# A load that is sent later and four warming products fewer, at the start of a hybrid encoder layer

## The chip, the cores and the metric

The kernel runs on one core of a Trainium2 chip. The metric is the device time of one execution in microseconds (us): 418.63 us, the median of three executions before the change (417.64 to 419.09). TensorE is called PE here, VectorE DVE, ScalarE ACT, GpSimd POOL and SyncE SP.

## The reference

One step of a streaming encoder layer for two groups of rows, 256 of a prompt and 32 of a running stream, all with the same weights. One projection of x feeds every branch:

```python
p = x @ w_in                                  # x: 288 x 1024 in all, w_in: 1024 x 11848
(qa, ka, va, oa, za, ia, fa, qb, kb, vb, zb, qi, ki, wi, ga, gb) = jnp.split(p, cuts, axis=-1)
...
score = jnp.einsum('bqh,bqhs->bqs', wi * (IDX_HEADS ** -0.5), jax.nn.relu(sc))   # sc: qi against ki
_, idx = lax.top_k(score, k_sel)
...
mixed = jax.nn.sigmoid(ga) * (branch_a @ w_out_a) + jax.nn.sigmoid(gb) * (branch_b @ w_out_b)
return layer_norm(DN_ALPHA * x + mixed @ w_o, ln_g, ln_b)
```

Branch A is an mLSTM with a matrix memory of 4 heads, branch B a sparse attention of 8 heads over the keys that the index scores pick. The change touches neither: it lies in the first microseconds, in the first part of `x @ w_in`.

## The kernel before

The weights come in tiles of 128 output columns (`ORDER` lists them). A weight tile is 128 partitions by 1024 float32. ACT rounds it to a high part (`wh`), DVE subtracts to get the low part (`wl`), and PE multiplies in three passes (high by high, high by x's low part, low by high), each 8 times over the 1024 rows of the sum in blocks of 128.

The first five tiles (the small tile `sm` and the four `qi` tiles) are handled apart, because they are what the start waits for. Their data and x come packed by block: for each of the 8 blocks k, `first[:, k]` holds 288 columns of x and then 5 x 128 weight columns, 928 in all. `lead[k]` is its place in SBUF. Block 0 comes in two pieces, cut behind the first weight tile (`cut` = 288 + 128 = 416 columns):

```python
    sp.dma_start(lead[0][:, 0:cut], a["first"][:, 0, 0:cut])
    act.dma_start(lead[0][:, cut:LEAD], a["first"][:, 0, cut:])
    for k in range(1, KT):
        sp.dma_start(lead[k][:, 0:LEAD], a["first"][:, k])
```

The first piece and the seven whole blocks go through SP's queue (q1 in the profile), the second piece through ACT's (q10). `first_products` (line 993 holds its one product) then runs, for every block, over the five tiles. Block 0 is multiplied as plain float32 from `lead[0]` as it landed, without splitting. The product with tile 0 reads the first piece alone, those with tiles 1 to 4 read the weights of the second piece and x of the first. Blocks 1 to 7 are split first (lines 181 to 192) and multiplied in three passes of five products.

Ahead of that PE runs `WARM` = 16 products of a zeroed tile (`warm`, bfloat16, 256 columns) whose result nobody reads (line 160). DVE clears that tile first (line 155).

Each engine executes its instructions in the order in which the program records them; what stands in one engine's queue waits for what is ahead of it. DMAs are issued in the order of the queue of the engine that issues them, and such an issue may carry a wait for another engine. The DMAs take eight semaphores in turn (DMAHW0 to DMAHW7); the ninth DMA waits until the first one's has been reached.

Of the kernel before, what the change touches and what calls it, by code (L numbers as in the profile page):

```python
# [12 lines left out]
BF = mybir.dt.bfloat16  # L13
# [12 lines left out]
BH, BD = 8, 128  # L26
IH, ID = 8, 64
CHUNK = 64
WARM = 16
MID = 4  # L30
FIRST = 5
LEAD = T + 128 * FIRST
# [55 lines left out]
def body(ctx, tc, a, o):  # L88
    nc = tc.nc
    pe, act, dve, pool, sp = nc.tensor, nc.scalar, nc.vector, nc.gpsimd, nc.sync  # L90
# [5 lines left out]
    def sb(name, shape, dt=F32, tag=None, bufs=1):  # L96
        return P.tile(shape, dt, name=name, tag=tag or name, bufs=bufs)

    def bank(name, n=512):
        return ps.tile([128, 512], F32, name=name, tag="side", bufs=6)  # L100
# [50 lines left out]

    xh = sb("xh", [128, KT, T], F32R)
    xl = sb("xl", [128, KT, T], F32R)
    warm = sb("warm", [128, 256], BF)
    dve.memset(warm, 0.0)
    wp = bank("warm_p")

    def keep_warm(n):
        for _ in range(n):
            pe.matmul(wp[:, :256], lhsT=warm[:, :128], rhs=warm, start=True, stop=True)  # L160

    keep_warm(WARM)

    early = sb("early", [128, 2064], tag="v1l")
# [5 lines left out]
    lead = [sb(f"wst_k{k}", [128, KT * 128], tag="wst", bufs=8) for k in range(KT)]  # L170
    cut = T + 128
    sp.dma_start(lead[0][:, 0:cut], a["first"][:, 0, 0:cut])
    act.dma_start(lead[0][:, cut:LEAD], a["first"][:, 0, cut:])
    for k in range(1, KT):
        sp.dma_start(lead[k][:, 0:LEAD], a["first"][:, k])
# [1049 lines left out]
```

## Time and profile before

| | us |
|---|---|
| median of the three timed executions | 418.63 (417.64 to 419.09) |
| the profiled execution, whole | 418.94 |
| its span, first to last instruction | 417.1 |
| PE busy | 410.7 (98% of the span) |
| DVE, ACT, POOL busy | 315.6, 214.6, 201.8 |
| DMA moved | 78.89 MB, mean 189 GB/s |

The span is what the trace covers; the 1.84 us that the whole execution takes beyond it are not in the trace. PE's busy share counts the warming products too. Times in the trace's rows are from the span's start.

### The profile page before, as it was taken

The page shows a single profiled execution, that of the slowest core. Times are in us where ns is not written, and L with a number is a line of the kernel's source. Part 1 is how long each engine was busy: PE and PEld are TensorE (multiplying, and loading weights), DVE is VectorE, ACT ScalarE, POOL GpSimd, SP SyncE. Part 2 cuts the span into 40 slices and gives each one's busy share as a digit, 9 for nine tenths or more (in the row PEclk, how much of TensorE's full clock was granted, in tenths as well). Part 3 has the DMA queues.
Part 4 walks back from the last instruction along what each step waited for, and adds up shares of the span by engine and source line. Part 5 has one row for each costly group of instructions (what it writes and reads, how often), then busy time and mean ns, then how long its engine had stood idle before and what let it go on. Part 6 is the DMA issues. An engine that isn't in the chain of part 4 may idle for free.

```text
span 417.1 us, 8481 instructions
## 1 busy us (share of the span) xinstructions
PE 410.7 (98%) x3145; PEld 392.9 (94%) x3145; DVE 315.6 (76%) x633; ACT 214.6 (51%) x408; POOL 201.8 (48%) x466
## 2 busy tenths in 40 slices
PE   8999999999999999999999999999999999999995
PEld 7999999999999998779999999999999999998864
DVE  4669999987887596778898788897565466666674
ACT  5776465344845565567554556455434333535402
POOL 0200049995288856857920164766615448710031
PEclk9999999999999999999999999999999999999999
DMA  8987878779844720448535643444555547444014
GB/s 308 394 286 224 285 238 295 274 194 330 308 145 152 242 91 0 166 145 306 172 122 163 234 135 128 150 154 152 194 160 158 193 153 263 158 152 126 25 48 143
DMA packets 32948, 78.89 MB, mean 189 GB/s; under 512 B 11644, under 2 KB 15084, under 8 KB 32108
## 3 DMA queue, kind: packets, MB, share of 16 engines
q1 hardware_dynamic: 32044, 77.05, 55.5%
q10 hardware_dynamic: 864, 1.32, 1.0%
q8 instruction: 24, 0.39, 0.4%
q14 instruction: 16, 0.13, 0.1%
HBM read 72.45 MB, written 7.81 MB: 192 GB/s over the span
## 4 chain that ended last, share of the span: by engine, by line
PE 97%; DVE 1%; POOLq 0%; ACT 0%; DVEq 0%; issue 0%
PE pj L930 25%; PE pj L931 25%; PE pj L932 24%; PE yn L974 5%; PE pj L993 4%; PE vap L946 1%; PE pj L948 1%; PE vap L953 1%; PE vap L947 1%; PE pj L947 1%; PE vap L948 1%; PE pj L946 1%; PE warm_p L160 1%; PE yn L978 1%; PE ix L406 1%; PE os L544 0%
## 5 line engine op out<-in xcount | busy, mean ns | idle before, releaser
L930 PE MATMUL pj<-xh,wh 128*128 128x288 f32 x640 | 189.2, 296 | 0.0
L931 PE MATMUL pj<-xl,wh 128*128 128x288 f32 x640 | 188.9, 295 | 0.0
L932 PE MATMUL pj<-xh,wl 128*128 128x288 f32 x640 | 188.6, 295 | 0.0
L149 DVE TENSOR_TENSOR wl<-wst,wh 128x1024 fp32r<-128x1024 f32 x112 | 138.0, 1234 | 28.0 <-ACT wh L142 27.6
L142 ACT CAST wh<-wst 128x1024 fp32r<-128x1024 f32 x112 | 117.4, 1048 | 22.8 <-PE pj L931 6.8
L930 PEld LDWEIGHTS pj<-xh,wh 128*128 128x128 f32 x640 | 120.3, 188 | 1.4 <-issue 1.3
L931 PEld LDWEIGHTS pj<-xl,wh 128*128 128x128 f32 x640 | 120.3, 188 | 0.0
L932 PEld LDWEIGHTS pj<-xh,wl 128*128 128x128 f32 x640 | 120.3, 188 | 0.0
L117 POOL COPY pt<-bm 32x96 f32<-32x96 f32 x128 | 50.4, 394 | 20.3 <-DVE bm L584 15.1
L117 POOL COPY kaT<-kn 32x128 f32<-32x128 f32 x64 | 32.1, 502 | 22.8 <-DVE kn L681 20.3
L117 POOL COPY hn<-qaT 32x128 f32<-32x128 f32 x48 | 24.1, 502 | 17.4 <-DVE qaT L657 10.2
L117 POOL COPY vn<-qaT 32x128 f32<-32x128 f32 x64 | 28.0, 438 | 2.6
L891 ACT ACTIVATE sg<-pj 128x288 f32<-128x288 f32 x16 | 6.6, 411 | 26.1 <-PE pj L932 26.1
L932 PE MATMUL pj<-bah,wl 128*128 128x288 f32 x64 | 18.9, 296 | 0.0
L931 PE MATMUL pj<-bbl,wh 128*128 128x288 f32 x64 | 18.9, 296 | 0.0
L931 PE MATMUL pj<-bal,wh 128*128 128x288 f32 x64 | 18.9, 295 | 0.0
L930 PE MATMUL pj<-bah,wh 128*128 128x288 f32 x64 | 18.8, 294 | 0.0
L932 PE MATMUL pj<-bbh,wl 128*128 128x288 f32 x64 | 18.8, 294 | 0.0
L930 PE MATMUL pj<-bbh,wh 128*128 128x288 f32 x64 | 18.8, 293 | 0.0
L738 POOL TENSOR_TENSOR dd<-dd,mhalf 128x2 f32<-128x2 f32 x4 | 5.4, 1350 | 24.6 <-DVE dd L737 24.4
L1024 POOL TENSOR_TENSOR nr<-mv,mhalf 128x1 f32<-128x1 f32 (+1 forms) x3 | 4.0, 1349 | 24.3 <-DVE mv L1023 24.3
L824 ACT CAST mxh<-sg 128x288 fp32r<-128x288 f32 x8 | 3.5, 433 | 22.7 <-DVE sg L904 22.7
(465 smaller groups left out, 717.8 us busy)
## 6 DMA issues: line engine op xcount, KB each, us to landing
wst<-in_w SPq DMA_DIRECT2D x112, 512.0 KB
wst_k<-in_first SPq DMA_DIRECT2D x7, 464.0 KB
rscr<-rrow SPq DMA_DIRECT2D x2, 768.0 KB
out_k<-kbT SPq DMA_DIRECT2D x1, 1152.0 KB
stC<-in_state_C SPq DMA_DIRECT2D x1, 1028.0 KB
out_C_sample<-stC SPq DMA_DIRECT2D x1, 1028.0 KB
bm<-rscr SPq DMA_DIRECT2D x1, 1024.0 KB
ckT<-in_cache_k SPq DMA_DIRECT2D x1, 1024.0 KB
```

What stands on the lines that cost most here:

```text
L117: pool.tensor_copy(out(quads[k], quads[i]), turned(quads[i], quads[k]))
L142: act.copy(split[t][0], stage[t])
L149: dve.tensor_tensor(wl, stage[t], wh.bitcast(F32), OP.subtract)
L891: act.activation(sg, q, AF.Sigmoid)
L930: pe.matmul(p[:, :T], lhsT=wh[:, c], rhs=h[:, k], start=(k == 0), stop=False)
L931: pe.matmul(p[:, :T], lhsT=wh[:, c], rhs=l[:, k], start=False, stop=False)
L932: pe.matmul(p[:, :T], lhsT=wl[:, c], rhs=h[:, k], start=False, stop=(k == KT - 1))
L946: pe.matmul(banks[i], lhsT=xh[:, k, r], rhs=wh[:, c], start=(k == 0), stop=False)
L947: pe.matmul(banks[i], lhsT=xh[:, k, r], rhs=wl[:, c], start=False, stop=False)
L948: pe.matmul(banks[i], lhsT=xl[:, k, r], rhs=wh[:, c], start=False, stop=(k == KT - 1))
L974: pe.matmul(p, lhsT=x[:, k, r], rhs=w[:, c], start=first and i == 0, stop=last and i == 2)
L993: pe.matmul(p[t][:, new], lhsT=w[:, 128 * t:128 * t + 128], rhs=x[:, new], start=(k == 0), stop=(k == KT - 1 and w is wl))
```

## The change

The warming products read a constant of ones that POOL sets in the program's preamble, and there are 12 of them. DVE's first instruction no longer clears `warm` (which is gone) but the place of the second piece in `lead[0]`; since the second piece is then written to the same place, its DMA, in ACT's queue, waits for DVE.

```diff
-WARM = 16
+WARM = 12
...
-    warm = sb("warm", [128, 256], BF)
-    dve.memset(warm, 0.0)
     wp = bank("warm_p")
+    ones = nc.const_aps.tensor(1.0, (128, 256), BF)

     def keep_warm(n):
         for _ in range(n):
-            pe.matmul(wp[:, :256], lhsT=warm[:, :128], rhs=warm, start=True, stop=True)
+            pe.matmul(wp[:, :256], lhsT=ones[:, :128], rhs=ones, start=True, stop=True)
...
     sp.dma_start(lead[0][:, 0:cut], a["first"][:, 0, 0:cut])
+    dve.memset(lead[0][:, cut:LEAD], 0.0)
     act.dma_start(lead[0][:, cut:LEAD], a["first"][:, 0, cut:])
```

ACT's queue at the program's start, before (`wst_k0` is `lead[0]`, `wst_k1` is `lead[1]`; the words in brackets are the semaphores that an instruction waits for):

```order
L173 DMA wst_k0_88<-in_first 128x512
L182 ACT_TABLE_LOAD
L182 CAST xh_65<-wst_k0_88 128x288 [waits DMAHW1_49]
L182 CAST xh_65<-wst_k1_89 128x288 [waits DMAHW2_49]
L191 CAST wh_k1_107<-wst_k1_89 128x384
```

And with the change:

```order
L173 DMA wst_k0_82<-in_first 128x512 [waits DVE_49]
L182 ACT_TABLE_LOAD
L182 CAST xh_65<-wst_k0_82 128x288 [waits DMAHW0_49]
L182 CAST xh_65<-wst_k1_83 128x288 [waits DMAHW1_49]
L191 CAST wh_k1_102<-wst_k1_83 128x384
```

The order is the same; the issue of the second piece has a wait for DVE, and the table load and the casts stand behind it. The first piece's semaphore is now DMAHW0 instead of DMAHW1.

PE's queue where the warming products end and block 0 begins, before:

```order
L160 LDWEIGHTS warm_67
L160 MATMUL warm_p_69<-warm_67 128x256
L993 MATMUL pj0_190<-wst_k0_88 128x288 [waits DMAHW1_49]
L993 MATMUL pj1_191<-wst_k0_88 128x224 [waits DMAHW0_49]
L993 MATMUL pj2_192<-wst_k0_88 128x224
L993 MATMUL pj3_193<-wst_k0_88 128x224
L993 MATMUL pj4_194<-wst_k0_88 128x224
L993 MATMUL pj0_190<-xh_65,wh_k1_107 128x288 [waits DVE_49,Activation_49]
```

And with the change:

```order
L159 LDWEIGHTS const-bfloat16-1.0
L159 MATMUL warm_p_67<-const-bfloat16-1.0 128x256
L993 MATMUL pj0_185<-wst_k0_82 128x288 [waits DMAHW0_49]
L993 MATMUL pj1_186<-wst_k0_82 128x224 [waits DMAHW2_49]
L993 MATMUL pj2_187<-wst_k0_82 128x224
L993 MATMUL pj3_188<-wst_k0_82 128x224
L993 MATMUL pj4_189<-wst_k0_82 128x224
L993 MATMUL pj0_185<-xh_65,wh_k1_102 128x288 [waits DVE_49,Activation_49]
```

The product with tile 0 waits for the first piece, the one with tile 1 for the second, in both; twelve pairs of a weight load and a product stand ahead of them instead of sixteen, and the first of these no longer waits for DVE.

SP's queue, which has the first piece and the blocks, with the change:

```order
L171 DMA wst_k0_82<-in_first 128x416
L175 DMA wst_k1_83<-in_first 128x928
L175 DMA wst_k2_84<-in_first 128x928
L175 DMA wst_k3_85<-in_first 128x928
L175 DMA wst_k4_86<-in_first 128x928
L175 DMA wst_k5_87<-in_first 128x928
L175 DMA wst_k6_88<-in_first 128x928
L175 DMA wst_k7_89<-in_first 128x928 [waits DMAHW0_49]
L131 DMA wst5_145<-in_w 128x1024 [waits DMAHW1_49,DMAHW2_49,DVE_49,PE_49]
```

The last block's load waits for DMAHW0 in both; that was the second piece's semaphore before and is the first piece's now. The first weight tile behind it (`wst5`) also waits for PE, which must have read `lead[0]`, whose place it takes.

## Rows read from the trace of the kernel before

**Rows 1.** The page: busy time and share of each engine (busy us, share of the span, instructions), and the chain that ended last, by engine.

```profile
PE 410.7 (98%) x3145; PEld 392.9 (94%) x3145; DVE 315.6 (76%) x633; ACT 214.6 (51%) x408; POOL 201.8 (48%) x466
...
PE 97%; DVE 1%; POOLq 0%; ACT 0%; DVEq 0%; issue 0%
```

**Rows 2.** All waits of PE in the whole span (us in total, times, longest), and busy time by stretch: the stretch, its length, then PE, PEld, DVE, ACT and POOL busy us with instructions, granted clock, DMA share, GB/s.

```profile
PE warm_p L160 <- DVE warm L155: 1.1, 1, 1.1
...
7.30:19.40 12.10, 12.10 (x106) 12.10 (x105) 9.67 (x15) 9.10 (x15) 1.19 (x10) 1.00 1.03 394
19.50:100.00 80.50, 80.50 (x640) 80.17 (x639) 71.64 (x164) 43.63 (x87) 40.75 (x92) 1.00 0.81 262
100.00:200.00 100.00, 100.00 (x797) 92.47 (x796) 77.22 (x170) 61.26 (x141) 66.55 (x168) 1.00 0.53 182
200.00:300.00 100.00, 100.00 (x776) 98.08 (x776) 83.50 (x174) 52.24 (x92) 49.79 (x100) 1.00 0.49 159
300.00:405.00 105.00, 104.92 (x764) 98.93 (x764) 64.71 (x97) 43.01 (x65) 40.47 (x88) 1.00 0.44 142
```

**Rows 3.** The start in order of time: start us, length us, engine, line, what, how many, and in brackets how long the engine had been idle and what ended it.

```profile
0.38 0.10 POOL L1203 MEMSET const-bfloat16-1.0<- 128x1 bf16 x1
...
0.80 0.41 ACTq L173 DMA_DIRECT2D wst_k<-in_first  x1
0.81 0.40 SPq L172 DMA_DIRECT2D wst_k<-in_first  x1
0.90 0.17 DVE L155 MEMSET warm<- 128x128 uint32 x1 [0.90 <-PEq L1203]
...
1.12 3.60 PE L160 MATMUL warm_p<-warm 128*128 128x256 bf16 x16 [1.12 <-DVE warm L155]
1.25 1.28 ACT L182 ACT_TABLE_LOAD   x1 [1.25 <-PEq L1203]
1.27 3.56 SPq L175 DMA_DIRECT2D wst_k<-in_first  x7
4.34 0.43 ACT L182 CAST xh<-wst_k 128x288 fp32r<-128x288 f32 x1 [1.81 <-DMA wst_k<-in_first]
```

**Rows 4.** PE's products one by one, from the last warming product to the first of block 1 (start us, length us as modelled with its end; the starts are what is read).

```profile
4.30 0.42 PE L160 MATMUL warm_p<-warm 128*128 128x256 bf16 x1
4.51 0.69 PE L993 MATMUL pj<-wst_k 128*128 128x288 f32 x1
5.00 0.69 PE L993 MATMUL pj<-wst_k 128*128 128x288 f32 x1
5.48 0.58 PE L993 MATMUL pj<-wst_k 128*128 128x224 f32 x1
5.85 0.58 PE L993 MATMUL pj<-wst_k 128*128 128x224 f32 x1
6.22 0.60 PE L993 MATMUL pj<-wst_k 128*128 128x224 f32 x2
6.47 0.54 PE L993 MATMUL pj<-wst_k 128*128 128x224 f32 x2
6.66 0.54 PE L993 MATMUL pj<-wst_k 128*128 128x224 f32 x2
6.85 0.54 PE L993 MATMUL pj<-wst_k 128*128 128x224 f32 x2
7.26 0.46 PE L993 MATMUL pj<-xh,wh_k 128*128 128x288 f32 x1
```

**Rows 5.** The length of DVE's memsets: all of line 155 (one, ns minimum, median and maximum), and line 300's by shape (busy us, mean ns).

```profile
L155 DVE MEMSET warm<- x1: 165/165/165, 0.9 to 0.9; 128x128 uint32 x1
...
L300 DVE MEMSET gt<- 4x576 f32 x1 | 0.5, 538 | 0.1
```

**Rows 6.** What the two DMA queues had moved by 2.9 us and by 3.5 us (packets, MB, share of 16 engines), with q1 the queue of SP and q10 that of ACT.

```profile
q1 hardware_dynamic: 65, 0.11, 16.1%
q10 hardware_dynamic: 43, 0.09, 14.3%
...
q10 hardware_dynamic: 103, 0.21, 22.1%
q1 hardware_dynamic: 123, 0.20, 20.4%
```

**Rows 7.** Stretches of the start (columns as in rows 2), for the DMA rate in the last column and the granted clock ahead of the DMA share.

```profile
1.80:2.40 0.60, 0.60 (x5) 0.41 (x4) 0.00 (x0) 0.60 (x1) 0.00 (x0) 1.00 0.86 127
2.40:2.90 0.50, 0.50 (x4) 0.38 (x3) 0.00 (x0) 0.13 (x1) 0.00 (x0) 1.00 0.73 240
3.40:3.90 0.50, 0.50 (x5) 0.33 (x3) 0.00 (x0) 0.00 (x0) 0.00 (x0) 1.00 1.14 428
4.40:5.60 1.20, 1.20 (x5) 0.91 (x4) 0.46 (x1) 0.37 (x1) 0.00 (x0) 1.00 1.06 424
```

**Rows 8.** SP's load of the last block, which waits for the second piece's semaphore, and the preparation of block 1 (ACT and DVE) in order of time.

```profile
4.50 0.33 SPq L175 DMA_DIRECT2D wst_k<-in_first  x1
...
5.61 0.43 ACT L182 CAST xh<-wst_k 128x288 fp32r<-128x288 f32 x1 [0.84 <-DMA wst_k<-in_first]
5.95 0.51 ACT L191 CAST wh_k<-wst_k 128x384 fp32r<-128x384 f32 x1
```

## The prediction

> **What bounds the kernel now.** I read the page first: PE is busy for 98% of the span and makes up 97% of the chain that ended last [rows 1]. Then PE's own waits: there is one in the whole span, the 1.12 us before its first product, and by stretch PE is busy without a break to 300 us and for 104.92 of the next 105 us [rows 2]. So every instruction of PE starts when the one before it lets it, and a shift of PE's work at the start is carried to the end, unless something that does not move with PE catches up with it. The other engines' work is released by PE (buffers come free when PE has read them), so it moves along. What counts is the moment at which PE is through with block 0.
>
> Then the start in order of time [rows 3]. SP and ACT issue the two pieces at 0.81 and 0.80. DVE clears the warming tile from 0.90, PE begins at 1.12 and runs 16 products; the starts of the first and the last are (4.30 - 1.12) / 15 = 0.212 us apart each [rows 3, 4]. The first piece has landed by 4.34, when ACT, idle until then, begins its cast [rows 3]. PE begins block 0 at 4.51, that is 0.21 after its last warming product: here it is the products that hold PE back, by 0.17 us, and not the data. The second piece had landed by 4.50, since SP's load of the last block, which waits for that semaphore, goes out then [rows 8]; PE wants it only at 5.48, behind the product with tile 0 (two entries of 0.49 us) [rows 4].
>
> The third thing is PE's clock. The product with 224 columns starts 0.37 us after the one before at 5.85 and at 6.22, and 0.19 us at 6.66 and 6.85 [rows 4]: the lower and the higher of the two levels, 1.2 and 2.4 GHz, with the rise between 6.22 and 6.47; I take 6.3. (The granted clock in the stretches reads 1.00 throughout [rows 7]; the products' own distance says otherwise, and I go by it.) PE had been busy without a break for 5.2 us when the clock rose. Until the rise, a microsecond gained at the start is worth half a microsecond at the end, because the work brought forward is then done at half rate.
>
> **The change part by part.**
>
> *The constant.* The wait for DVE goes. The constant is set by POOL at 0.38, before the barrier [rows 3], so PE can start when the barrier lets it: not before 0.80, where ACT and SP start, and not after 1.12. I take DVE's 0.90. A product of 128x256 that reads one column over and over is not in the trace; it costs 0.212 us if it goes like the zeroed tile's, and could cost 0.25 before the next step is touched.
>
> *Four products fewer.* 12 x 0.212 = 2.54 us from 0.90: PE is free at 3.45 instead of 4.51.
>
> *The memset.* 128 elements took 165 ns and 576 took 538 [rows 5]: 0.83 ns for one more, so 512 take about 0.48 us. DVE ends at 1.38 and ACT's issue, at 0.80 before, goes out at about 1.45: 0.65 us later. DVE's next work was at 4.80, behind ACT's cast; nothing is queued there that waits. On ACT the table load stands behind the issue: from 1.25-2.53 it moves to about 1.9-3.2. The cast of the first piece, at 3.7 at the earliest below, covers that; were the cover gone, the cast would feed only block 0's split x, which no product of block 0 reads. On SP nothing is queued behind the new wait. The last block's load now waits for the first piece instead of the second, so it goes out no later, and behind six blocks it finds DMA at its full rate [rows 7].
>
> *The first piece alone.* By 2.9 us the two queues had moved 0.11 and 0.09 MB, by 3.5 us 0.20 and 0.21 [rows 6]; the first piece is 0.213 MB, so it was through at about 3.55. Now the second begins 0.65 later, at about 2.6. If SP's queue alone then gets what both got, it has 127 GB/s x 0.6 us + 240 x 0.2 = 0.124 MB at 2.6 [rows 7]; for the other 0.09 MB it gets half of some 300 GB/s and needs 0.6 us: 3.2, or 0.35 earlier, and the landing moves from 4.34 to 4.0. The ends: no gain at all, 4.34, if a single queue is no faster alone; and 0.6 us, 3.7, if it shares nothing. I take 4.0. PE then waits from 3.45 to 4.0 and does tile 0 until 4.97.
>
> *The second piece.* It starts 0.65 later and now meets block 1 in SP's queue. Between 2.9 and 3.5 the queues moved 58 and 60 packets [rows 6], the same number; block 1's rows are 928 x 4 = 3712 bytes against 512 x 4 = 2048, so ACT's queue should get 2048 / 5760 = 36% of 0.42 MB/us, 0.15. At 3.2 it has about 0.09 of its 0.262 MB; the rest takes 1.15 us, to 4.35. Before, by the same arithmetic (0.21 at 3.5, then 55% of 0.428 [rows 7]), it ended at 3.7 and landed at 4.50. That is later by 0.65, the whole delay; if it keeps half of the rate it is through at 4.0, later by 0.3. I take 0.6, near the first: landed at 5.1. The ends are 4.5, no later than before, and 5.3. Block 1 itself had to share with the second piece in both kernels, so that its landing (ACT's cast at 5.61 [rows 8]) stays where it is.
>
> *The sum.* PE begins tile 1 at the later of 4.97 and 5.1, so at 5.1 instead of 5.48: 0.38 earlier. With the clock's rise at 6.3 as before that is worth half: 0.19 us, say 0.2. With the ends: a first piece at 4.34 gives 5.31 and 0.09; a second piece at 5.3 the same; a first piece at 3.7 and a second by 4.67 gives 0.8 earlier, 0.4 us. Block 1 is ready for it: the high weights are done at 5.95 + 0.51 = 6.46 [rows 8] and PE comes at about 7.07 instead of 7.26. So 417.1 - 0.2 = 416.9 for the span, and 418.74 with the 1.84 us around it. The profiled execution lay 0.31 above the median; from the median the same gain gives 418.4.
>
> **The rivals.**
>
> *The clock rises later (slower).* The new thing in the trace will be two gaps of PE, 0.55 us at 3.45 and 0.13 at 4.97, in the stretch in which before it was busy for 5.2 us on end and then was given the higher clock. If the gaps count as a break, the 5.2 us begin anew at 4.0 (rise at 9.2) or at 5.1 (10.3). From tile 1 on, PE has then done (9.2 - 5.1) / 2 = 2.05 us of work at 9.2, where before it had done 9.2 - 6.3 + (6.3 - 5.48) / 2 = 3.3: 1.25 us later, 419.9; with a rise at 10.3, 1.8 us, 420.4. It decides as soon as the gap delays the rise by more than 0.4 us. For it: no other row shows PE idle at this point. Against it: the gaps are short beside the work around them. The Trainium skill (TensorE: Matmul & The Clock Gate, HAM oscillation — how this bites in real kernels) describes waits for DMA between groups of products that bring the clock back down; its waits are far longer than the gaps here, and no row before has such a gap. The sum by it is the one of this rival.
>
> *Nothing (no change).* The second piece eats what the first gains: it lands at 5.3 or later, PE begins tile 1 about when it did, 418.5 to 418.7. For it: the delay of 0.65 us is nearly the 0.98 us for which the second piece lay unused, and the queue it meets has larger packets. Against it: even the delay in full leaves 0.3 us.
>
> *The clock rises earlier.* PE begins 0.2 us earlier, and the rise might come a good deal earlier as well. Then block 0 is through sooner, but block 1's high weights, ready at 6.46, are the next bound: 0.8 us before 7.26, so 417.8 at the best. Against it: nothing in the rows says that the rise follows the first product so closely. The same skill page (What's actually happening) says that the rise is not tied to the program's start and falls differently from run to run. One profile cannot show that; the three times, 1.45 us apart, would fit it, and by it the medians of two unchanged kernels could differ by some tenths.
>
> **How the numbers follow.** 0.45 for the forecast (418.4, its own range 418.0 to 418.7), 0.25 for nothing, 0.16 for the later rise, 0.14 for the earlier one. About 0.3%, 1.26 us here, is what a measurement of this kernel can tell from no change. The forecast and nothing lie inside it. The earlier rise stops at 0.8 us and passes it only if the median falls low as well: faster 0.04. The later rise gives 1.25 to 1.8 us, past it in over half of its cases: slower 0.10. The range reaches from the earlier rise with some of the spread, 417.6, to just under the lower end of the later rise, 419.8.
>
> **What would show it.** In the changed kernel's trace: PE's first product between 0.8 and 1.1 and the twelfth at about 3.2; ACT's issue at about 1.45; ACT's first cast (the first piece) at about 4.0; tile 1's first product at about 5.1, idle time before it put down to a DMA; the distance of 224-column products halving at about 6.3; block 1's first product at about 7.07. A halving later than 6.7 is the first rival; a tile 1 that begins after 5.4 is the second. The prediction is wrong if the first cast is not earlier than 4.2, or if PE has waits behind block 0.

## The result and the profile after

The change made the kernel slower: 422.44 us against 418.37, medians of nine executions each, a ratio of 1.0079 (95% interval 1.0059 to 1.0099). The times also spread more: 418.76 to 423.38, where those of before lie between 417.60 and 419.09. The profiled execution took 423.05 us, its span 421.3, that is 4.2 over the span of before. (Here and below a ratio is not the quotient of the two medians beside it, which would be 1.0097 here; it lies near that of the means.)

The page after, busy time by engine and the chain that ended last by engine, against [rows 1]:

```profile
PE 412.7 (98%) x3141; PEld 394.3 (94%) x3141; DVE 316.2 (75%) x633; ACT 214.7 (51%) x408; POOL 203.6 (48%) x466
...
PE 95%; DMA 1%; DVE 1%; POOLq 0%; ACT 0%; DVEq 0%; issue 0%
```

PE is busy 2.0 us longer with four products fewer, and a DMA now stands in the chain, which had none. PE's waits in the whole span, against the first line of [rows 2]:

```profile
PE pj L993 <- DMA wst_k<-in_first: 2.6, 1, 2.6
PE warm_p L159 <- PEq L1203: 0.8, 1, 0.8
```

One wait, for one of block 0's pieces. The start in order of time, against [rows 3] and [rows 8]:

```profile
0.81 0.39 SPq L171 DMA_DIRECT2D wst_k<-in_first  x1
0.84 2.72 PE L159 MATMUL warm_p<-const-bfloat16-1.0 128*128 128x256 bf16 x12 [0.84 <-PEq L1203]
0.98 0.48 DVE L172 MEMSET wst_k<- 128x512 f32 x1 [0.98 <-PEq L1203]
1.26 4.08 SPq L175 DMA_DIRECT2D wst_k<-in_first  x7
1.50 0.38 ACTq L173 DMA_DIRECT2D wst_k<-in_first  x1
...
3.33 0.43 ACT L182 CAST xh<-wst_k 128x288 fp32r<-128x288 f32 x1
3.35 1.32 PE L993 MATMUL pj<-wst_k 128*128 128x288 f32 x2
5.44 0.43 ACT L182 CAST xh<-wst_k 128x288 fp32r<-128x288 f32 x1 [1.68 <-DMA wst_k<-in_first]
7.30 3.36 PE L993 MATMUL pj<-wst_k 128*128 128x224 f32 x8 [2.62 <-DMA wst_k<-in_first]
```

Up to 3.4 us all goes as the change meant it. PE starts at 0.84 instead of 1.12; the first piece is there at 3.33 instead of 4.34, just as the twelve products end. Then tile 0 is done, and PE waits for the second piece until 7.30. Block 1, issued at 1.26 by SP, is there at 5.44 (ACT's next cast), well ahead of the second piece of block 0.

What the two queues had moved by 3.5, by 4.1 and by 5.0 us in the changed kernel, against [rows 6]:

```profile
q1 hardware_dynamic: 204, 0.44, 42.3%
q10 hardware_dynamic: 2, 0.00, 0.4%
...
q1 hardware_dynamic: 258, 0.63, 50.0%
q10 hardware_dynamic: 5, 0.01, 0.7%
...
q1 hardware_dynamic: 301, 0.74, 46.9%
q10 hardware_dynamic: 108, 0.21, 11.7%
```

By 4.1 us ACT's queue (q10) had moved 5 packets and SP's 258 (144 of them for the first piece), though ACT's issue had ended at 1.88. From 3.5 to 4.1 it is 3 against 54, while block 1 is under way. Only then does the second piece come: from 4.1 to 5.0 it is 103 packets for ACT's queue and 43 for SP's, which had issued block 2 at 1.72. So the piece went behind block 1 and mostly ahead of block 2, in the order of the issues (1.26, 1.50, 1.72). Its last packets took until about 7. In the trace's semaphore records a DMA of this size reports in sixteen parts; thirteen of the second piece's had come by 5.63, the last three at 6.19, 6.99 and 7.25.

PE's products one by one, against [rows 4]:

```profile
8.95 0.58 PE L993 MATMUL pj<-wst_k 128*128 128x224 f32 x1
9.33 0.95 PE L993 MATMUL pj<-wst_k 128*128 128x224 f32 x2
10.15 0.75 PE L993 MATMUL pj<-xh,wh_k 128*128 128x288 f32 x1
11.52 0.47 PE L993 MATMUL pj<-xl,wh_k 128*128 128x288 f32 x1
12.61 0.47 PE L993 MATMUL pj<-xh,wl_k 128*128 128x288 f32 x1
13.52 0.75 PE L993 MATMUL pj<-xh,wh_k 128*128 128x288 f32 x5
14.10 0.74 PE L993 MATMUL pj<-xl,wh_k 128*128 128x288 f32 x5
```

The 224-column products of block 0 are 0.38 apart to the end (8.95, 9.33), the lower of the two levels of the clock. A pass of five products takes 1.09 us from 11.52 to 12.61 and 0.58 from 13.52 to 14.10: the clock rises near 13, where it had risen at 6.3 before. The trace's own records of the granted clock agree: the one at full clock begins at 6.34 before and at 13.29 here. (Ahead of it no record stands, and the stretches of [rows 7] print 1.00 there.)

From these starts the 4.2 us can be divided; block 2's first pass before is needed with them:

```profile
9.14 0.74 PE L993 MATMUL pj<-xh,wh_k 128*128 128x288 f32 x5
```

Tile 1 begins at 7.30 instead of 5.48: 1.82. From there to block 1's first product it is 10.15 - 7.30 = 2.85 instead of 7.26 - 5.48 = 1.78: 1.07 more, all of it the clock. From block 1 to the end of the span it is 421.3 - 10.15 = 411.15 instead of 409.84: 1.31 more. That is block 1's passes at the low clock: from its first product to block 2's it takes 13.52 - 10.15 = 3.37 instead of 9.14 - 7.26 = 1.88, 1.49 more, and from block 2 to the end there is no loss (407.78 against 407.96). So 1.8 us are the wait, and 2.4 the clock. In all thirteen traces of this document the stretch from block 2's first product to the end takes 407.7 to 408.1 us: the start alone decides, to within 0.4 us, how long a traced execution takes.

### The profile page after: what moved, and what is told of

It is laid out like the page before. It is cut to its first block, busy times and chain, and to the rows that moved or that the text cites. A ratio compares the mean times of both kernels' runs of the same rounds, so it can differ in the third digit from the quotient of the medians.

```text
span 421.3 us, 8473 instructions
## 1 busy us (share of the span) xinstructions
PE 412.7 (98%) x3141; PEld 394.3 (94%) x3141; DVE 316.2 (75%) x633; ACT 214.7 (51%) x408; POOL 203.6 (48%) x466
## 4 chain that ended last, share of the span: by engine, by line
PE 95%; DMA 1%; DVE 1%; POOLq 0%; ACT 0%; DVEq 0%; issue 0%
PE pj L930 24%; PE pj L931 24%; PE pj L932 24%; PE yn L974 5%; PE pj L993 4%; DMA wst_k<-in_first 1%; PE vap L946 1%; PE vap L953 1%; PE pj L948 1%; PE vap L947 1%; PE pj L947 1%; PE vap L948 1%; PE pj L946 1%; PE yn L978 1%; PE ix L406 0%; PE os L544 0%
```

## The experiments

Two theories after this trace. A: the second piece's lateness costs it all, by the wait and by the clock that the wait keeps low. B: the four products that are missing cost most of it, since PE's work ahead of the data no longer raises the clock. The edits are given against the changed kernel. What an experiment's times spread over is told with its median, since the spread turned out to matter.

**The second piece without the wait, 12 products.**

```diff
-    dve.memset(lead[0][:, cut:LEAD], 0.0)
```

> The changed kernel without the memset of the second piece's place, so that ACT sends the piece at once as before; the constant and the 12 warming products stay. Theory A (the late second piece costs it all: PE waits for it 2.6 us, and the wait keeps the clock low until 13 us): the pieces land at 4.3 and 4.5 us as before, PE waits some 0.9 us before block 0, tile 1 begins at about 5.3, the clock rises between 6 and 8, and the time is 418.0 to 419.0 us, within 0.2% of before. Theory B (four warming products fewer cost most of it, because PE's work ahead of the real products no longer raises the clock; the late piece costs only the 1.8 us by which tile 1 begins later): the clock rises at 10 us or later and the time is 420 to 421 us.

Measured: a median of 417.91 us, a ratio to before of 1.0005 (0.9984 to 1.0026). But the ten times fall in two heaps, with nothing between them: six from 417.44 to 417.92, four from 419.68 to 420.79. The profiled one is of the upper heap (419.98):

```profile
4.44 4.32 PE L992 MATMUL pj<-wst_k 128*128 128x288 f32 x10 [0.88 <-DMA wst_k<-in_first]
8.25 1.29 PE L992 MATMUL pj<-xh,wh_k 128*128 128x288 f32 x5
9.38 0.74 PE L992 MATMUL pj<-xl,wh_k 128*128 128x288 f32 x5
9.96 0.74 PE L992 MATMUL pj<-xh,wl_k 128*128 128x288 f32 x5
```

PE idles 0.88 us ahead of block 0, whose data come as in the kernel before (4.44). Block 0 then takes 3.81 us instead of 2.75, and the pass that begins at 8.25 still takes 1.13: the clock rises near 9.1. A comes near the median, B holds for four times in ten. Neither is the whole. Only one execution of the upper heap was traced, so that the rise is what parts the two heaps is inferred here.

**Sixteen products, the wait kept.**

```diff
-WARM = 12
+WARM = 16
```

> The changed kernel with 16 warming products in place of 12; the second piece still waits for the memset. Theory A: the second piece lands at about 7.3 us as in the changed kernel, PE idles from about 5.2 to 7.3, the clock rises at 10 to 13 us, 421.5 to 422.8 us. Theory B: the clock rises near 6.3 as before, only the wait is left: 418.4 + 1.4 = 419.8 us.

Measured: 419.08 us (418.52 to 422.28), a ratio of 1.0035 (1.0013 to 1.0057). Less than either theory expected, with two times near 422. In its trace PE does tile 0 at 4.21 and waits 0.8 us instead of 2.6, the products behind the wait come at the higher clock, and block 1 begins at 7.26 as before:

```profile
5.80 1.78 PE L993 MATMUL pj<-wst_k 128*128 128x224 f32 x8 [0.80 <-DMA wst_k<-in_first]
7.26 0.89 PE L993 MATMUL pj<-xh,wh_k 128*128 128x288 f32 x5
```

So the second piece lands at quite different times, 5.8 here and 7.3 in the changed kernel's trace. Four more products shorten the idle stretch. In this trace the clock had risen at 4.49 (the record's begin), before the wait; that the four products brought it there is not shown, since the kernel before, with as many, has its rise at 6.34.

**Products in the wait.**

```diff
                     pe.matmul(p[t][:, new], lhsT=w[:, 128 * t:128 * t + 128], rhs=x[:, new],
                               start=(k == 0), stop=(k == KT - 1 and w is wl))
+                    if k == 0 and t == 0:
+                        keep_warm(12)
```

> The changed kernel with 12 more warming products between block 0's product with tile 0 and the one with tile 1, where PE waits for the second piece (12 x 0.212 = 2.5 us against a wait of 2.6). Theory A: the piece still lands at about 7.3, but PE is busy while it waits and the clock rises between 6 and 8; what is left is tile 1's later begin, 7.3 against 5.48 less the half rate before, about 1.4 us over before: 419.5 to 420.2 us. If the clock does not depend on the idle stretch: no gain, 422 to 423 us.

Measured: 419.52 us (418.52 to 421.09), a ratio of 1.0034 (1.0018 to 1.0050), as A expected; 2.9 us of the changed kernel's 4.1 are gone. In its trace, the slowest of the ten executions, tile 1 begins even later, and yet:

```profile
7.94 1.78 PE L993 MATMUL pj<-wst_k 128*128 128x224 f32 x8 [1.16 <-DMA wst_k<-in_first]
9.40 0.46 PE L993 MATMUL pj<-xh,wh_k 128*128 128x288 f32 x1
```

The eight records of tiles 1 to 4 take 9.40 - 7.94 = 1.46 us, all at the higher clock, where the changed kernel needs 2.85. The work is the same; what differs is what PE did in the wait, and the clock's record begins at 6.09, amid the added products. It then stays up through a wait of 1.16 us.

**Both pieces in SP's queue.**

```diff
-    dve.memset(lead[0][:, cut:LEAD], 0.0)
-    act.dma_start(lead[0][:, cut:LEAD], a["first"][:, 0, cut:])
+    sp.dma_start(lead[0][:, cut:LEAD], a["first"][:, 0, cut:])
```

> The changed kernel with the second piece in SP's queue, right behind the first and ahead of block 1, without the memset and without a wait; the constant and 12 warming products stay. Theory A (the piece was late because it stood behind the blocks of SP's queue): the first piece lands at about 3.3 to 3.6, the second at 4.4 or earlier, PE has no wait of over 0.3 us behind tile 0, the clock rises between 6 and 8, and the time is 417.6 to 418.4 us. Theory B: the clock rises at 10 us or later, 420 us or more. If the second piece is late for another reason (its engine's place, not the queue): it lands after 5 us here too.

Measured: 419.63 us (418.98 to 420.33), a ratio of 1.0031 (1.0020 to 1.0042): slower than before, which no theory expected. The pieces were early (tile 0 at 3.35, and PE goes on to tile 1 without a wait), but now block 1 is late, and PE waits for it:

```profile
7.20 0.43 ACT L181 CAST xh<-wst_k 128x288 fp32r<-128x288 f32 x1 [3.46 <-DMA wst_k<-in_first]
...
7.68 1.01 PE L992 MATMUL pj<-xh,wh_k 128*128 128x288 f32 x5 [1.01 <-ACT xh L181]
```

Block 1 lands at 7.20 instead of 5.61. That the pieces' order of bytes would be the whole story is refuted; why block 1 lags with a single queue stays open. Of its sixteen parts the first came at 4.91, half by 5.51 and the last two at 6.75 and 7.18, so here too it is the last parts that are late.

**A shorter head start.** The memset covers 64 of the 512 columns; DVE's part shrinks to 0.11 us, and ACT's issue goes out at 1.03.

```diff
-    dve.memset(lead[0][:, cut:LEAD], 0.0)
+    dve.memset(lead[0][:, cut:cut + 64], 0.0)
```

> The changed kernel with a memset of 64 of the second piece's 512 columns: by 0.83 ns a column it is 0.37 us shorter, so ACT's issue goes out at about 1.14 us, just ahead of SP's issue of block 1 (1.26), instead of 1.50. Theory Q (the DMA engines drain what stands in SP's queue before they turn to ACT's, so that what counts is which issue comes first): the second piece lands at 4.3 to 4.8, PE waits under 0.5 us behind tile 0, and the time is 417.5 to 418.6 us. Theory E (ACT's queue is served late as soon as the first piece has a head start, whatever block 1 does): the piece lands after 5.2, 419 us or more.

Measured: 418.23 us (417.84 to 418.92), a ratio of 1.0003 (0.9993 to 1.0012). The loss is gone, as Q expected. By 3.5 us the second piece has moved 0.22 MB (0.00 in the changed kernel), PE does tile 0 at 3.56 and has no wait behind it:

```profile
q1 hardware_dynamic: 147, 0.22, 24.8%
q10 hardware_dynamic: 111, 0.22, 18.2%
...
1.03 0.38 ACTq L173 DMA_DIRECT2D wst_k<-in_first  x1
1.26 3.86 SPq L175 DMA_DIRECT2D wst_k<-in_first  x7
...
3.56 2.56 PE L993 MATMUL pj<-wst_k 128*128 128x288 f32 x10
5.93 1.00 PE L993 MATMUL pj<-xh,wh_k 128*128 128x288 f32 x5
8.28 0.84 PE L993 MATMUL pj<-xh,wh_k 128*128 128x288 f32 x5 [0.19 <-ACT wh_k L191]
```

From 2.9 to 3.5 us the order of the changed kernel is turned round: 101 packets for ACT's queue, 22 for SP's. The traced execution is the fastest of the ten, and its clock rises at 3.76, earlier than in any other trace.

**The same start for block 1.** A second memset, of 16 columns of block 1's place, makes SP's issue wait too.

```diff
     dve.memset(lead[0][:, cut:LEAD], 0.0)
+    dve.memset(lead[1][:, 0:16], 0.0)
```

> The changed kernel with a second, small memset (16 columns of block 1's place) behind the first, so that SP's issue of block 1 waits for DVE as well and goes out at about 1.55 us, beside the second piece's. Theory Q: with neither ahead the two share, as the two pieces did before: the second piece lands at 4.7 to 5.3, block 1 at 5.7 to 6.2, PE waits 0.2 to 0.8 us behind tile 0, and the time is 418 to 419.2 us. Theory E: the piece lands after 6 here too, 420 us or more.

Measured: 420.67 us (418.71 to 422.38), a ratio of 1.0051 (1.0032 to 1.0071). The issues went out side by side, at 1.50 and 1.52. What the queues had moved by 4.1 us, and what they moved from 3.5 to 4.7 us, and PE's first products of tile 1 and of block 1:

```profile
q1 hardware_dynamic: 224, 0.51, 47.6%
q10 hardware_dynamic: 40, 0.08, 5.7%
...
q1 hardware_dynamic: 81, 0.30, 66.3%
q10 hardware_dynamic: 72, 0.15, 32.5%
...
5.86 1.78 PE L994 MATMUL pj<-wst_k 128*128 128x224 f32 x8 [1.20 <-DMA wst_k<-in_first]
7.32 0.90 PE L994 MATMUL pj<-xh,wh_k 128*128 128x288 f32 x5
```

The 224 of SP's queue hold the 144 of the first piece, which had no rival; once both transfers are under way, from 3.5 to 4.7, the queues move 81 and 72 packets, nearly the same number, as Q says of issues at one time. Q's times are missed all the same: the wait is 1.20 us, not 0.2 to 0.8, and the median is 1.5 us above its range.

The traced execution is the fastest of the ten (418.71), and it shows that an idle stretch does not always put the clock's rise off. PE had 12 products and then idled 1.20 us behind tile 0, but the eight records of tiles 1 to 4 take 7.32 - 5.86 = 1.46 us, all at the higher clock, whose record begins at 5.16, within the idle stretch. The second trace of the changed kernel (below) has a shorter wait (0.88) and an earlier tile 1 (5.58), a rise at 9.29, and takes 420.18. Seven of the ten times here lie from 420.16 to 422.38; that they had a late rise is likely, but none of them was traced.

**A memset of 256 columns.** ACT's issue at 1.23, where 1.29 was expected: just ahead of SP's 1.26.

```diff
-    dve.memset(lead[0][:, cut:LEAD], 0.0)
+    dve.memset(lead[0][:, cut:cut + 256], 0.0)
```

> The changed kernel with a memset of 256 of the 512 columns: ACT's issue at about 1.29 us, just behind SP's issue of block 1 (1.26), 0.21 us earlier than in the changed kernel and 0.26 later than in the variant with 64 columns. Theory Q (which issue comes first decides): the second piece is served behind block 1 as in the changed kernel and lands at 5.2 us or later, 420 us or more. If the landing goes with the length of the delay: about 4.5 to 4.8 us, 418 to 419 us.

Measured: a median of 418.41 us, a ratio of 1.0011 (0.9995 to 1.0028), again in two heaps: six times between 417.98 and 418.46, four between 420.06 and 420.57. Its trace, of the upper heap, has tile 1 at 5.73 after a wait of 0.91, and the clock rises at 9.46. The expected order was not met, so it does not test an issue behind block 1's. With 0.03 us between the issues the two queues again share: from 2.9 to 4.1 us ACT's moved 80 packets and SP's 64. An issue 0.20 us later than in the variant with 64 columns was enough to bring the wait back in this execution.

**No wait and no gap.** Without the memset, and 17 products, which reach to the first piece's landing.

```diff
-WARM = 12
+WARM = 17
...
-    dve.memset(lead[0][:, cut:LEAD], 0.0)
```

> The changed kernel without the memset (the second piece goes at once) and with 17 warming products of the constant: they run from 0.84 to about 4.45, to where the first piece lands, so PE has no gap. If the gap ahead of block 0 is what split the times of the variant with 12 products and no wait into 417.4 to 417.9 and 419.7 to 420.8, no time here is over 419.3, and the median is 417.9 to 418.4, up to 0.3 us under before since PE starts 0.28 earlier. If the split has another cause (the constant, or the pieces' landing), times near 420 stay.

Measured: 418.19 us (417.47 to 419.05), a ratio of 0.9999 (0.9990 to 1.0009). The upper heap of the variant with 12 products is gone, as expected, by these ten times: it goes with the 0.88 us in which PE was idle, not with the constant and not with the landing, which are nearly the same in both (block 0 begins at 4.56 here and at 4.44 there).

**No wait and a long gap.** Without the memset, and 4 products.

```diff
-WARM = 12
+WARM = 4
...
-    dve.memset(lead[0][:, cut:LEAD], 0.0)
```

> The changed kernel without the memset (the second piece goes at once, pieces at about 4.4 and 4.6 us) and with only 4 warming products: PE is idle from about 1.7 to 4.4 us, as long as the changed kernel's PE is idle behind tile 0, but no product of block 0 begins later than in the variant with 12 products and no wait. What it is slower by is then the clock's rise alone. Theory A2 (the idle stretch, wherever it lies ahead of the rise, puts the rise off, and that is the larger part of the loss): the rise falls at 8 to 11 us, 419.8 to 421.3 us. If the clock is not moved by the idle stretch: 418 to 419 us.

Measured: 419.94 us (419.60 to 420.99, five executions), a ratio of 1.0042 (1.0027 to 1.0057). The waits, and PE's passes:

```profile
PE pj L992 <- DMA wst_k<-in_first: 2.6, 1, 2.6
...
4.43 4.31 PE L992 MATMUL pj<-wst_k 128*128 128x288 f32 x10 [2.58 <-DMA wst_k<-in_first]
8.23 1.16 PE L992 MATMUL pj<-xh,wh_k 128*128 128x288 f32 x5
9.23 0.74 PE L992 MATMUL pj<-xl,wh_k 128*128 128x288 f32 x5
```

Here block 0 begins at 4.43, earlier than the 4.51 of before, and PE is idle only where before it worked on zeros. What it loses is the clock: block 0 takes 3.80 us instead of 2.75, and the clock rises near 8.8. Between this trace and that of before it is 1.25 us at block 2's first product (10.39 against 9.14), between the medians 1.6. An idle stretch as long as the changed kernel's, at a place where it delays no work, costs this much.

**The changed kernel again.**

> The changed kernel once more, for a second trace of it: the second piece lands between 5.3 and 8 us, over 0.8 us behind its place before; PE's wait behind tile 0 is its landing less 4.3 to 4.7; the clock rises at 8 us or later; 419 to 423.4 us. If the late piece of the first trace was a single mishap, it lands under 5.2 here and the time is under 419.

Measured: 421.99 us (418.38 to 423.66), a ratio of 1.0072 (1.0048 to 1.0097). Its profiled execution took 420.18, less than the median, with a span of 418.4:

```profile
5.58 3.36 PE L993 MATMUL pj<-wst_k 128*128 128x224 f32 x8 [0.88 <-DMA wst_k<-in_first]
8.42 1.30 PE L993 MATMUL pj<-xh,wh_k 128*128 128x288 f32 x5
9.56 0.74 PE L993 MATMUL pj<-xl,wh_k 128*128 128x288 f32 x5
```

This time the second piece is there at 5.58, and tile 1 begins only 0.10 us later than before. From tile 1 to block 1 it is 2.84 us instead of 1.78, so 1.06 more, and from block 1 to the end 409.98 instead of 409.84. Nearly all of the 1.3 us by which this span is longer is the clock (its record begins at 9.29), and the wait as such costs a tenth. So the long landing of the first trace is not needed for a loss; it makes it larger.

**The two good parts together.** The memset of 64 columns and 13 products.

```diff
-WARM = 12
+WARM = 13
...
-    dve.memset(lead[0][:, cut:LEAD], 0.0)
+    dve.memset(lead[0][:, cut:cut + 64], 0.0)
```

> The variant with the short memset (64 columns, ACT's issue at about 1.03 us, ahead of block 1) and 13 warming products instead of 12, so that they reach to about 3.6 us, where the first piece has landed. Theory (the early piece is worth something only while the clock is low, and block 1, ready at about 6.3, bounds the rest): 417.8 to 418.3 us, 0 to 0.1% under before. If the head start is worth what it brings block 0 forward (over 1 us): 417.5 or less.

Measured: 418.39 us (417.40 to 418.73), a ratio of 0.9995 (0.9986 to 1.0004). No measurable gain over before. In its fastest execution, the one traced, block 1 begins at 5.99 instead of 7.26, but its median is that of before. That execution has its rise at 4.61, against 6.34 in the trace of before; how much of its gain is the early piece and how much the early rise is open, as no execution near the median was traced. No variant beat the kernel before.

## Why the prediction was wrong

Forecast were 418.4 us and a range to 419.8; measured were 422.44. The range missed, and the sign with it. Neither of the two signs that were to show it wrong came: the first cast was early (3.33), and PE had no wait behind block 0. What came were the signs of two of its rivals, tile 1 after 5.4 (7.30) and the clock's rise after 6.7 (13.29).

The bound of the kernel was read rightly: PE stays without a wait behind block 0, and a shift of its work at the start goes through to the end, since from block 2 on the traces are alike within 0.4 us. The small terms held: the memset took 0.48 us as worked out from [rows 5], ACT's issue went out at 1.50 (1.45 forecast), PE began at 0.84 (0.90) and the products of the constant cost the same as those of zeros. The table load behind the issue, the last block's load and the casts cost nothing.

**The first piece** came earlier than its better bound, 3.33 against 3.7: alone, SP's queue lost nothing to the other, since by 3.5 us ACT's had moved two packets.

**The second piece** is the step that failed. The prediction took from [rows 6] that two queues get the same number of packets, and set the landing at 5.1 with 5.3 as the worst. Those rows show two transfers issued within 0.01 us of each other. With SP's block 1 issued 0.24 us earlier, ACT's queue got 3 packets to SP's 54 from 3.5 to 4.1 us, and the piece was used at 7.30 in one trace and 5.58 in another. A share read from two issues at one time was carried to an issue that follows another, and the bound was built on the same share, so it was no bound. The variants bear this out: with the piece's issue ahead (64 columns) PE has no wait for it, and with both issues at one time the queues share again. An estimate with block 1 as a whole ahead of the piece, at the 0.42 MB/us that the prediction used, gives a landing at about 5.5 (0.44 of the 0.69 MB of the first piece and block 1 were through by 3.5, so the rest is at 4.1 and the piece at 4.7, and 0.8 to the landing as before). That is near the 5.58 of the second trace. The 7.30 of the first lies beyond it, by three of the piece's sixteen parts, and why they came late is open.

**The clock** was named as a rival, with its mechanism, at 0.16 and a price of 1.25 to 1.8 us. The mechanism was right, and the runs put it at the centre: 2.4 of 4.2 us in the first trace, nearly all of 1.3 us in the second, 1.6 us between the medians in the variant in which it stands alone. It was given too little weight because the gaps were taken as short (0.55 and 0.13 us); the gap was 2.62. The variant with 12 products and no wait shows in its trace that even 0.88 us can go with a late rise (9.1), and its times suggest it for four executions of ten; 1.20 us did not in the trace with block 1 held back. The sentence of the Trainium skill's page (TensorE: Matmul & The Clock Gate, HAM oscillation — how this bites in real kernels), that waits for DMA between groups of products bring the clock down, was set aside because its waits are longer. No run here shows a clock brought down at the start: in the trace with products in the wait it stayed up through 1.16 us. What the traces show is a rise that came late, from 8.8 to 13.3 us, in five of the six in which PE was idle for 0.88 to 2.62 us before it had come.

**The rival that nothing changes** priced a late second piece at zero, since it counted only tile 1's begin. The wait has two prices, and the second, by way of the clock, was left out there.

**The earlier rise** had its bound too late: block 1 was to wait for its high weights until 6.46, but begins at 5.93 in the variant with 64 columns and at 5.99 with 13 products, because its first two tiles need only the columns that DVE casts. In the first of these the preparation of block 2 then makes PE wait (0.19 us at 8.28). Both are the fastest execution of their kernel, with an early rise (3.76 and 4.61). The medians of these two variants, the best that the change could have done, lie within 0.1 us of that of before.

## What to carry to other kernels

Work that holds PE busy ahead of the data should reach to the moment when the data are there, also where one product's data come in two transfers: 17 products without a gap gave one narrow heap of times, 12 with a gap of 0.88 us two, 4 with one of 2.58 us a median 1.6 us higher. One trace says little about it, since the rise differs from execution to execution. A transfer held back by a few tenths of a microsecond can lose its place to what another queue issues in between, here the 0.475 MB of block 1, so the price of a delay is to be counted from that work and not from the delay. And a forecast that costs a wait should cost the clock behind it too, wherever the clock has not yet risen.

## What the runs showed of the hardware

- Two queues issued together moved about as many packets each: 58 and 60 packets from 2.9 to 3.5 us with the issues 0.01 us apart [rows 6], 81 and 72 from 3.5 to 4.7 us with 0.02 us, 64 and 80 (SP's and ACT's) from 2.9 to 4.1 us with 0.03 us. With issues 0.23 to 0.24 us apart the earlier was served nearly alone: 54 to 3 from 3.5 to 4.1 us with SP's ahead, 22 to 101 from 2.9 to 3.5 us with ACT's ahead. Where between 0.03 and 0.23 us the one passes into the other was not measured.
- Of the same program, two traces show the second piece in use at 7.30 and at 5.58. In the first, ACT's queue had moved 0.21 MB of 0.26 by 5.0 us and the rest took two microseconds more. Of the sixteen parts in which the DMA reports, the last three came from 6.19 to 7.25; in the second trace all had come by 5.53.
- Both pieces in SP's queue brought the pieces early and block 1 1.6 us late (7.20 against 5.61), with its sixteen parts spread from 4.91 to 7.18. The cause of such stragglers is open.
- The rise of the clock differs from execution to execution. In the seven traces in which PE was hardly idle (under 0.3 us at a time) between its first product and the rise, it came at 3.76, 4.49, 4.61, 5.56, 6.09, 6.34 and 6.80 us. In the other six PE was idle for longer; it came at 8.80 (2.58 us idle), 9.10 and 9.29 (0.88), 9.46 (0.91) and 13.29 (2.62), but once at 5.16, within an idle stretch of 1.20. That the upper heaps of times are the executions with a late rise fits these traces, but there is none from the lower heap of a kernel whose upper heap has one.
